# Two-layer diffusion backbone on one core: context halves of the gated tiles and the retention's token tiles moved by 192 bytes, output tiles taken in twos, weight casts tied behind two copies

## The chip, the cores and the metric

The kernel runs on one core of one Trainium2 chip. The metric is the device time of one execution in microseconds (us), as the median of several runs. A core has a matrix engine (TensorE, PE in the profile, with its weight loads listed as PEld), a vector engine (VectorE, DVE), a scalar engine (ScalarE, ACT), a general engine (GpSimd, POOL) and a queue that issues most DMAs (SyncE, SP). Each engine works through its own list of instructions in order and waits at an instruction until the semaphores that it needs have come.

## The reference

Two layers over 512 latent tokens (`x`) and 256 context tokens (`ctx`), width 1024, float32. Layer 0 mixes tokens by windowed attention, layer 1 by bidirectional chunkwise retention with four heads. Each layer ends with the same kind of feed-forward block, of width 2816, that is, 22 feature tiles of 128:

```python
def swiglu(h, w_in, w_out):
    gate, up = jnp.split(h @ w_in, 2, axis=-1)
    return (jax.nn.silu(gate) * up) @ w_out

for i in range(DEPTH):                      # DEPTH = 2
    need_ctx_out = i < DEPTH - 1            # the context leaves the net after layer 0
    h_x, h_c = modulate(rms_norm(x, ...)), modulate(rms_norm(y_ctx, ...))
    out_c, out_x = windowed_gqa_sink(...) if i % 2 == 0 else bidir_retention(...)
    x = x + mx[2] * out_x
    x = x + mx[5] * swiglu(modulate(rms_norm(x, norm2_g[i]), mx[3], mx[4]), ffn_w_in[i], ffn_w_out[i])
    if need_ctx_out:
        y_ctx = y_ctx + mc[2] * out_c
        y_ctx = y_ctx + mc[5] * swiglu(modulate(rms_norm(y_ctx, ...), mc[3], mc[4]), ffn_w_in[i], ffn_w_out[i])
```

So the first feed-forward block works on 512 latent and 256 context tokens, the second one on the 512 latent tokens alone, and the retention's projections work on the latent tokens and read the context's.

## The kernel before

**Products in three.** Every float32 number is held as two parts of a reduced type: a rounded one ("hi", a ScalarE copy that casts) and the rest ("lo", a VectorE subtraction). `split` makes both; `mm3` multiplies them as three matmuls, hi·hi, lo·hi and hi·lo. A weight tile is loaded by SP into a `wraw` buffer and split into `whi` and `wlo` (`next_w`, `w_parts`). Of `wraw` there are two buffers in the pool `rp`; SP's next load into one of them waits until the split of what it held is over.

**Layout.** Each pool of tiles lies at consecutive addresses of a partition, pools on the left and on the right are stacked against each other, and within a pool the tags follow each other in the order of their first use. The sizes are multiples of 256 bytes nearly everywhere. Tiles that start at a multiple of 256 bytes are called on the grid here. `off_grid(pool, cols)` puts a filler of 48 or 16 columns (192 or 64 bytes) into a pool, and so moves the tiles behind it, or on the right side those in front of it, by 192 bytes past the grid; a filler of the other size puts what follows back on it. In the kernel before, the operands of the second feed-forward block (`hx`, `sA`), the token sums of the retention (`sA` in the pool `hS`) and the context's normed tokens (`hc`) stand 192 bytes past the grid; the gated parts of the first feed-forward block (`act`) and the retention's own tokens (`aq` in the pool `hR`: `h_first`, four tiles with the first 256 tokens of the first four feature tiles, and `h_rest`, eight tiles) stand on it.

**First feed-forward block** (lines 879 to 1155, about 380 to 895 us). The 22 feature tiles come in groups of 2, 4, 4, 4, 4 and 4. From the third tile on, `seven` makes gate and up projection with seven quarter products over 384 columns each instead of eight (the 768 tokens are two halves of 384: latent 0 to 383, then latent 384 to 511 with the 256 of the context). `finish_half` multiplies gate and up of one half and splits the product into a part of the tile `act`, which holds hi in columns 0 to 767 and lo in columns 768 to 1535. After the first tile of a group, `output` multiplies the tiles of the group before with `w_out`: for each of the 8 output tiles `d` first the 512 latent columns into a `pj` bank, then the 256 context columns into a `Z` bank, each followed by `gated_add` on VectorE (line 256). One weight tile serves `1024 / (128 * tiles of the group)` output tiles. The last group's output runs all latent tiles first and then all context tiles. Between them `ada_next` hands VectorE one or two sums for the layer-1 modulation, whose weights GpSimd's queue loads.

**Retention** (lines 1159 to 1662). For every head `product_q` streams tokens as the moving operand (256 columns) past weights, and `product_v` streams weights (512 columns) past the tokens as the stationary operand; `quarter_of` says which tiles "11", "12" and "22" (the tokens themselves) and 1 to 4 (the sums) are.

**Second feed-forward block** (lines 1669 to 1785, about 1400 to 1744 us). The same groups, for 512 latent columns. `seven` runs its products in this order: "11" into bank Y, 1 into Z, 2 added to Y, "12" into X, 3 added to Y, 4 added to Z, "22" added to Y. Four ScalarE copies take intermediate states out of the banks: `p1` (line 1720) after "11", `z1` (1722) after 1, `u2` (1724) after 2, `u3` (1729) after 3; product 2 cannot start before `p1` is out of Y. Right after the `p1` copy, `act_parts` splits the gated tile of the seven before. `output` of the group before follows the first `seven` of a group, with four weight tiles for groups of four; the last group's output follows the 22nd tile.

**Order.** The program gives the order in which work is traced; a planner then orders each engine's instructions with estimates of its own for how long each instruction and transfer takes, so a ready instruction may pass one that it thinks is not ready. `after(ins, others)` forbids `ins` to be put ahead of `others` on its engine, and adds no semaphore.

Of the kernel before, what the change touches and what calls it, by code (L numbers as in the profile page):

```python
# [9 lines left out]
F32R = mybir.dt.float32r  # L10
# [4 lines left out]
P = 128  # L15
D = 1024
KT = D // P
SX = 512
SC = 256
# [5 lines left out]
FFN_GROUPS = (2, 4, 4, 4, 4, 4)  # L25
# [24 lines left out]
def dit_kernel(ctx, tc, xT, cT, crow, small, consts, masks, tabs0, tabs1, jtab, adaQ, adaN, adaT, wst, out):  # L50
    nc = tc.nc
# [10 lines left out]
    def T(pool, cols, tag, bufs, dt=F32):  # L62
        return pool.tile([P, cols], dt, tag=tag, bufs=bufs, name=tag)
# [56 lines left out]
    def w_raw(pool=None, bufs=2):  # L120
        raw = T(pool or rp, 1024, "wraw", bufs)
        nc.sync.dma_start(raw, wst[wpos[0]])
        wpos[0] += 1
        return raw

    def w_parts(pool, own=2):

        bufs = own
        if ring:
            pool, bufs = ring[wsel[0] % len(ring)], 2  # L130
        elif wsel[0] % (2 + own) < 2:
            pool, bufs = rp, 2
        wsel[0] += 1
        return T(pool, 1024, "whi", bufs, F32R), T(pool, 1024, "wlo", bufs, F32R)

    def next_w(pool, own=2, raw=None, behind=(), late=()):

        raw = raw or w_raw()
        w = w_parts(pool, own)
        after(split(raw, *w, behind), late)  # L140
        return w
# [21 lines left out]
    def split(t, hi, lo, behind=()):  # L163
        after(nc.scalar.copy(hi, t), behind)  # L164
        return nc.vector.tensor_tensor(lo, t, hi, op=sub)  # L165
# [57 lines left out]
    hpool = [None, None]  # L223
# [4 lines left out]
    def off_grid(pool, cols):  # L228

        nc.gpsimd.memset(T(pool, cols, "off%d" % cols, 1), 0.0)  # L230
# [597 lines left out]
    for g in range(NKV):  # L828
        final = g == NKV - 1
        for i, (s, b) in enumerate((latent + context, latent + context, mixed, late)[g]):  # L830
# [4 lines left out]
            if (g, i) >= SPLIT_AT:  # L835
# [3 lines left out]
                if first:  # L839
                    wo0 = wpos[0]  # L840
                    cres = load_stream(1)
# [5 lines left out]
    xr = load_stream(0)  # L847
# [2 lines left out]
    PLAIN = 2  # L850
    WIDE = SX + SC
    THIRDS = (slice(0, 384), slice(384, WIDE))
    E = ExitStack()
    ep = E.enter_context(tc.tile_pool(name="ep", bufs=1, reuse_waits="tile"))
    wo_p = A.enter_context(tc.tile_pool(name="wo", bufs=1, reuse_waits="tile"))
    wsel[0] = 2
    ada_wo = [(part, d) for part in (3, 4) for d in range(4, KT)]
    for d4 in range(0, KT, 4):
        wpos[0] = wo0 + max(d4, 2)
        w = [next_w(wo_p) if d > 1 else wo_w[d] for d in range(d4, d4 + 4)]  # L860
# [42 lines left out]
    fp = F.enter_context(tc.tile_pool(name="fp", bufs=1, reuse_waits="tile"))  # L903
    quarter = lambda: T(hq, 768, "aq", 20, F32R)
    parts = lambda t: (t[:, 0:384], t[:, 384:768])
    bank = lambda n: T(psF, 512, n, 2)[:, 0:384]
    fp32 = [T(ep, 2 * WIDE, "act", 5) for _ in range(4)]
    tm = [fp32[k % 4][:, k // 4 * WIDE:(k // 4 + 1) * WIDE] for k in range(KT)]
    A = {(k, 0): parts(T(ep, 768, "aq", 8, F32R)) for k in range(KT)}
    A.update({(k, 1): parts(quarter()) for k in range(KT)})  # L910
# [1 line left out]
    def latent_shape():  # L912

        h1 = THIRDS[0]
        for k in range(KT):
# [8 lines left out]
    def context_shape(behind):  # L924
        rms(1, behind=behind)
        for k in range(KT):
            for s, c in ((0, slice(384, SX)), (1, slice(SX, WIDE))):
# [6 lines left out]
                else:  # L934
                    after(ins, [last_shape])
            split(tm[k][:, THIRDS[1]], *A[k, 1])

    park = T(fp, 2048, "crow", 1)

    def token_sums():  # L940

        h1, h2 = THIRDS
        for k in range(4):
# [18 lines left out]
               **{n: (lambda k, n=n: S[n, k]) for n in (1, 2, 3, 4)}}  # L962

    def new_act():
        return T(ep, 2 * WIDE, "act", 5, F32R)

    def finish_half(a, i, t, up):
        nc.vector.tensor_tensor(t, t, up, op=mult)
        c = THIRDS[i]
        return split(t, a[:, c], a[:, c.start + WIDE:c.stop + WIDE])  # L970

    def project_half(w, i, tag):
        o = bank(tag)
# [76 lines left out]
        silu(c21, Y)  # L1050
        return a, finish_half(a, 1, c21, c22)

    streams = ((0, xr, slice(0, SX)), (1, cres, slice(SX, WIDE)))
    ctx_sum = []

    def square_and_stats(s, d, t):
# [18 lines left out]
    def output(acts, final):  # L1075
        gsz = len(acts)
        nd = 1024 // (gsz * P)
        w = []

        def one(s, res, c, d):  # L1080
            while len(w) * nd <= d:
                w.append(spare_w() if final and len(w) == 2 else next_w(fp, 1, raw_turn()))
            wd = w[d // nd]
            o = bank("X" if final else "Z")[:, 0:SC] if s else pj()
            for k in range(gsz):
                c0 = k * nd * P + (d % nd) * P
                mm3(o, (wd[0][:, c0:c0 + P], wd[1][:, c0:c0 + P]),
                    (acts[k][:, c], acts[k][:, c.start + WIDE:c.stop + WIDE]), k == 0, k == gsz - 1)
            ins = gated_add(s, 0, 5, d, o, res)
            if cr and not final and s == 0 and d % 2:  # L1090
                ada_next(ins)
            if final:
                square_and_stats(s, d, res[d])

        if final:
            for st in streams:
                for d in range(KT):
                    one(*st, d)
        else:
            for d in range(KT):  # L1100
                for st in streams:
                    one(*st, d)

    def unit(u):
        w = [T(hq, 768, "aq", 20)[:, 0:512] for _ in range(KT - 4 * (u == 11))]
# [9 lines left out]
    ada_q = [t for i, both in enumerate(ada_both) for t in (both, *ada_one[2 * i:2 * i + 2])]  # L1115
    wsel[0] = 0
    raws = [0]
    cr = None
    last_shape, shape_end = latent_shape()
    first = first_two([next_w(fp, 1), next_w(fp, 1)], [next_w(fp, 1, late=[shape_end]), spare_w([shape_end])])  # L1120
# [4 lines left out]
    f, prev = 0, None  # L1125
    for gsz in FFN_GROUPS:
        acts = []
        for i in range(gsz):
            if f < PLAIN:
                acts.append(first[f])  # L1130
                if f == 1:
                    ends.pop(0)()
            else:
                if f == PLAIN:
                    last_sum()
                a, end = seven()
                acts.append(a)
                if f == PLAIN:
                    ends.pop(0)()
                if f == 4:  # L1140
                    cr = cond_rows(fp)
                if f > 3 and (i or f == 6):
                    ada_next(end)
            if i == 0 and prev is not None:
                output(prev, False)
            f += 1
        prev = acts
# [7 lines left out]
    F.close()  # L1155
    E.close()

# [8 lines left out]
    hS = H.enter_context(tc.tile_pool(name="hS", bufs=1, reuse_waits="tile", side="right"))  # L1166
# [5 lines left out]
    hpool[1] = qp  # L1172
    off_grid(qp, 48)
    h_sum = [(T(hS, 512, "sA", 16, F32R), T(hS, 512, "sA", 16, F32R)) for _ in range(KT)]
    off_grid(hS, 16)
    h_first = [T(hpool[0], 512, "aq", 12, F32R) for _ in range(4)]
    h_rest = [(T(hpool[0], 512, "aq", 12, F32R), T(hpool[0], 512, "aq", 12, F32R)) for _ in range(4)]
    chunk_base = wpos[0]

    def chunk(i, own=False):  # L1180
# [159 lines left out]
    for hd in range(RH):  # L1340
# [24 lines left out]
        Y, X, kc = W4("Y"), W4("X"), W4("X")  # L1365
# [219 lines left out]
        w = []  # L1585
# [82 lines left out]
    fp = F.enter_context(tc.tile_pool(name="fp", bufs=1, reuse_waits="tile"))  # L1668
# [36 lines left out]
    def seven():  # L1705
        g, u = w_raw(fp, 2), w_raw()
        b11 = w_parts(fp, 4)
        b22 = T(hM, 512, "hm", 8, F32R), T(hM, 512, "hm", 8, F32R)
        b14, b32 = w_parts(fp, 4), w_parts(fp, 4)
        split(g, *b11, norm_end)  # L1710
        split(u[:, 512:1024], *b22, norm_end)
        quarter_sums(g, u, first_end[1:2])
        split(u, *b32, first_adds)
        split(g, *b14, first_adds)
        X, Y, Z = (T(psF, 512, n, 2)[:, 0:SC] for n in "XYZ")
        t, up = t_hn(SX), t_sq(SX)
        e1, e2 = T(rp, 512, "res", 12), T(rp, 512, "res", 12)
        p1, z1, u2, u3 = e1[:, HALVES[0]], e1[:, HALVES[1]], e2[:, HALVES[0]], e2[:, HALVES[1]]
        product(Y, operand_a("11"), b11, 0, True)
        act_parts([nc.scalar.copy(p1, Y)])  # L1720
        product(Z, operand_a(1), b14, 0, True)
        nc.scalar.copy(z1, Z)
        product(Y, operand_a(2), b32, 512, False)
        nc.scalar.copy(u2, Y)
        product(X, operand_a("12"), b11, 512, True)
        nc.vector.tensor_tensor(t[:, HALVES[0]], p1, X, op=add)
        silu(t[:, HALVES[0]], t[:, HALVES[0]])
        product(Y, operand_a(3), b32, 0, False)
        nc.scalar.copy(u3, Y)
        product(Z, operand_a(4), b22, 0, False)  # L1730
        nc.vector.tensor_tensor(up[:, HALVES[0]], u2, Z, op=add)
        product(Y, operand_a("22"), b14, 512, False)
        nc.vector.tensor_tensor(up[:, HALVES[1]], u3, z1, op=add)
        silu(t[:, HALVES[1]], Y)
        nc.vector.tensor_tensor(t, t, up, op=mult)
        act = new_act()
        pending.append((t, *act))
        return act

    pending = []  # L1740

    def act_parts(behind=()):
        while pending:
# [2 lines left out]
    def output(acts, final):  # L1746
        gsz = len(acts)
        nd = 1024 // (gsz * P)
        w = []
        for d in range(KT):  # L1750
            while len(w) * nd <= d:
                w.append(next_w(fp, 4))
            wd = w[d // nd]
            o = pj()
            for k in range(gsz):
                c0 = k * nd * P + (d % nd) * P
                mm3(o, (wd[0][:, c0:c0 + P], wd[1][:, c0:c0 + P]), acts[k], k == 0, k == gsz - 1)
            ins = gated_add(0, 1, 5, d, o, xr)
            if len(first_adds) < 2:
                first_adds.append(ins)  # L1760
                after(first_mult[2], [ins])
            if final:
                nc.sync.dma_start(out[:, d, :], xr[d])
# [3 lines left out]
    for gsz in FFN_GROUPS:  # L1767
        acts = []
        for i in range(gsz):
            if f < 2:  # L1770
                acts.append(first[f])
            elif f == 2:
                w = [next_w(fp, behind=norm_end) for _ in range(2)]
# [155 lines left out]
```

## Time and profile before

| what | us |
|---|---|
| three runs | 1748.04 median, 1747.25 to 1749.0 |
| the profiled execution: its own time | 1746.27 |
| span of the profiled execution | 1744.5 |
| TensorE busy in the span | 1706.8 (98%) |
| VectorE busy | 1351.3 (77%) |
| ScalarE busy | 847.1 (49%) |

The granted TensorE clock is 0.999 of full speed. The profile's first part gives busy times by engine, its fourth the chain of work that ended last, its fifth groups of equal instructions. A row of groups reads: line, engine, operation, tile written and tiles read, shape, count, then busy time and mean duration of one in ns, then the idle time of the engine just before them and what ended it. A row of the timeline reads: start, duration, engine, line, operation, tiles, shape, count, and in brackets idle time before it with what ended it. A matmul's duration includes some 165 ns in which the next one already runs, so its rate is read from start to start.

### The profile page before, as it was taken

To read this page: it belongs to the slowest core of one execution; us is meant where nothing else is said; L and a number is where in the kernel's file an instruction comes from. 1 tells how busy PE (TensorE), PEld (TensorE's weight loads), DVE (VectorE), ACT (ScalarE), POOL (GpSimd) and SP (SyncE) were. 2 spreads that over 40 slices of the span, in tenths; PEclk is the share of its full clock that TensorE was granted. 3 is DMA by queue.
4 is the path that set the end of the run, shared out by engine and by line. 5 is a ranking of instruction groups with operands and counts; after the bars stand their busy time and mean duration, and the time that the engine had idled before them with its cause. 6 is when DMAs were issued, how large, how long until landed. Compare 5 with 4: busy or idle time off the path is not lost.

```text
span 1744.5 us, 27601 instructions
## 1 busy us (share of the span) xinstructions
PE 1706.8 (98%) x10876; PEld 1516.0 (87%) x10876; DVE 1351.3 (77%) x2368; ACT 847.1 (49%) x1492; POOL 132.2 (8%) x272
## 2 busy tenths in 40 slices
PE   7999999999999999999999999999999999999998
PEld 5777877899999999999988788898898899989987
DVE  6687778788778788787889858858768798877774
ACT  5476667455433334342556534525525565445442
POOL 0034435000000000000000000000000000000000
PEclk9999999999999999999999999999999999999999
DMA  9501012534243434343433524524423224233322
GB/s 350 233 13 38 13 43 68 198 120 142 71 147 121 158 109 145 122 151 103 154 102 87 181 76 132 166 82 125 160 86 114 80 79 133 80 113 106 106 76 85
DMA packets 59603, 203.54 MB, mean 117 GB/s; under 512 B 6609, under 2 KB 6993, under 8 KB 59217
## 3 DMA queue, kind: packets, MB, share of 16 engines
q1 hardware_dynamic: 51984, 175.03, 30.2%
q0 software_dynamic: 7200, 26.22, 4.9%
q8 instruction: 85, 1.39, 0.3%
q10 hardware_dynamic: 288, 0.52, 0.1%
q14 instruction: 46, 0.37, 0.1%
HBM read 199.65 MB, written 2.10 MB: 116 GB/s over the span
## 4 chain that ended last, share of the span: by engine, by line
PE 70%; DVE 14%; DMA 7%; ACT 4%; issue 3%; POOL 1%; SPq 0%; ACTq 0%; DVEq 0%; POOLq 0%
PE Y L886 13%; PE pj L147 6%; PE pj L148 6%; PE pj L149 6%; PE Z L886 6%; DMA wraw<-in_wst_dram 4%; PE Z L1270 4%; PE X L886 3%; DVE wlo L165 3%; PE pT L726 2%; PE pO L740 2%; PE S L703 2%; ACT whi L164 1%; PE X L1259 1%; PE Y L1259 1%
## 5 line engine op out<-in xcount | busy, mean ns | idle before, releaser
L164 ACT CAST whi<-wraw 128x1024 fp32r<-128x1024 f32 x258 | 270.2, 1051 | 373.1 <-PE Z L149 86.9
L165 DVE TENSOR_TENSOR wlo<-wraw,whi 128x1024 fp32r<-128x1024 f32 x258 | 315.3, 1225 | 61.7 <-ACT whi L164 59.1
L886 PE MATMUL Y<-aq,whi 128*128 128x384 f32 x640 | 173.7, 335 | 0.3 <-ACT hn L1035 0.3
L256 DVE SCALAR_TENSOR_TENSOR res<-pj,mod,res 128x512 f32<-128x512 f32 (+1 forms) x112 | 81.6, 730 | 64.9 <-PE pj L149 64.4
L886 PEld LDWEIGHTS Y<-aq,whi 128*128 128x128 f32 x640 | 116.7, 188 | 1.6 <-ACT hn L1035 1.4
L273 DVE CUSTOM_DVE_ANT_0 y<-adaw,crow,small_sb 128x1024 bf16<-128x1024 f32 x64 | 82.0, 1281 | 38.6 <-DMA adaw<-in_adaT_dram 38.3
L886 PE MATMUL Y<-aq,wlo 128*128 128x384 f32 x320 | 107.0, 334 | 0.0
L101 ACT ACTIVATE pr<-pr,stat,qs 128x513 f32<-128x513 f32 (+2 forms) x96 | 74.4, 777 | 22.8 <-DVE stat L710 22.2
L1270 PE MATMUL Z<-whi,sA 128*128 128x512 f32 x256 | 81.6, 393 | 1.6 <-ACT gate L1456 1.6
L717 POOL TENSOR_SCALAR pr<-pr,stat 128x512 f32<-128x512 f32 (+2 forms) x96 | 71.2, 755 | 78.7 <-DVE stat L714 54.0
L147 PE MATMUL pj<-ax,whi 128*128 128x512 f32 x176 | 68.7, 391 | 0.9 <-DVE res L256 0.9
L149 PE MATMUL pj<-ax,whi 128*128 128x512 f32 x176 | 68.7, 390 | 0.0
L148 PE MATMUL pj<-ax,wlo 128*128 128x512 f32 x176 | 68.6, 390 | 0.0
L147 PE MATMUL pj<-act,whi 128*128 128x512 f32 x168 | 66.0, 393 | 0.0
L148 PE MATMUL pj<-act,wlo 128*128 128x512 f32 x168 | 65.9, 392 | 0.0
L149 PE MATMUL pj<-act,whi 128*128 128x512 f32 x168 | 65.5, 390 | 0.0
L270 POOL DMA_DIRECT2D adaw<-in_adaT_dram x48 | 25.6, 533 | 514.6 <-DVE mod L273 413.1
L886 PE MATMUL Y<-sA,whi 128*128 128x256 f32 x304 | 59.1, 280 | 4.8 <-ACT res L1720 4.1
L726 PE MATMUL pT<-const_sb,pr 128*128 128x128 f32 x352 | 57.0, 283 | 6.9 <-POOL pr L717 4.6
L886 PEld LDWEIGHTS Y<-aq,wlo 128*128 128x128 f32 x320 | 60.1, 188 | 0.0
L726 PEld LDWEIGHTS pT<-const_sb,pr 128*128 128x128 f32 x352 | 38.5, 140 | 24.2 <-POOL pr L717 13.6
L1270 PEld LDWEIGHTS Z<-whi,sA 128*128 128x128 f32 x256 | 48.0, 188 | 13.2 <-ACT gate L1456 2.8
(576 smaller groups left out, 5141.8 us busy)
## 6 DMA issues: line engine op xcount, KB each, us to landing
wraw<-in_wst_dram SPq DMA_DIRECT2D x224, 512.0 KB, 3.7
adaw<-in_adaT_dram POOLq DMA_DIRECT2D x48, 512.0 KB, 3.8
wx<-in_wst_dram SPq DMA_DIRECT2D x30, 512.0 KB, 4.3
adan<-in_adaQ_dram SPq DMA_DIRECT2D x16, 512.0 KB, 7.8
adan<-in_adaN_dram SPq DMA_DIRECT2D x12, 512.0 KB, 7.6
adaw<-in_adaT_dram SPq DMA_DIRECT2D x8, 512.0 KB, 3.8
res<-in_xT_dram SPq DMA_DIRECT2D x14, 256.0 KB, 3.1
aq<-in_adaN_dram SPq DMA_DIRECT2D x12, 256.0 KB, 5.8
```

The costliest lines, as they stand in the source:

```text
L101: ins = nc.scalar.activation(*args, **kw)
L147: nc.tensor.matmul(o, whi, xhi, start=first, stop=False)
L148: nc.tensor.matmul(o, wlo, xhi, start=False, stop=False)
L149: return nc.tensor.matmul(o, whi, xlo, start=False, stop=last)
L164: after(nc.scalar.copy(hi, t), behind)
L165: return nc.vector.tensor_tensor(lo, t, hi, op=sub)
L256: return nc.vector.scalar_tensor_tensor(res[d], o, mods[l, s][:, part, d:d + 1], res[d], mult, add)
L273: res.append(nc.vector.tensor_tensor_reduce(junk, w, cr[:, s * 1024:(s + 1) * 1024], 1.0, sm_t[:, C_ADAB + l * 48 + j:C_ADAB + l * 48 + j ...
L717: nc.gpsimd.tensor_scalar(pt[:, :n], pt[:, :n], st[:, 6 + e:7 + e], 1.0, op0=mult, op1=mult)
L726: nc.tensor.transpose(tp[:, a * P:(a + 1) * P], self.pr[(0, 2, 1, 3)[a]][:, ki * P:(ki + 1) * P], ident)
L886: nc.tensor.matmul(o, p, r, start=first and k + i == 0, stop=k == 3 and i == 2, skip_group_check=not first)
L1270: ins = nc.tensor.matmul(os[t], p, r, start=first and k + i == 0, stop=k == 3 and i == 2, skip_group_check=by_k or not first)
```

## The change

Four edits:

1. The tile `act` of the first feed-forward block grows from 1536 to 1600 columns. The latent tokens' hi and lo parts lie in columns 0 to 511 and 512 to 1023; the context's hi and lo parts follow at column 1024 in the first tile of a group, and 48 columns (192 bytes) further in the others. `finish_half` of the second half therefore makes two splits, of 128 and of 256 columns, where it made one of 384.
2. `output` of that block, except for the last group, takes the output tiles in twos: the latent parts of two tiles, then the context parts of the same two.
3. In the retention's pool `hR` the 64-byte filler that stood in the pool `hS` now stands behind eleven `aq` tiles: all of `h_rest` and the last three tiles of `h_first` get 192 bytes past the grid, `h_first[0]` gets a tag of its own and stays on it, and the tiles of `hS` stay where they were.
4. In the second feed-forward block, `output` may put the cast of its first weight tile only behind the `z1` copy and that of the second one only behind the `u2` copy of the seven traced before it.

```diff
+    ACT = 1600
...
-    fp32 = [T(ep, 2 * WIDE, "act", 5) for _ in range(4)]
+    fp32 = [T(ep, ACT, "act", 5) for _ in range(4)]
...
     def new_act():
-        return T(ep, 2 * WIDE, "act", 5, F32R)
+        a = T(ep, ACT, "act", 5, F32R)
+        c0 = 2 * SX + 48 * (made[0] > 0)
+        made[0] = (made[0] + 1) % made[1]
+        return (a[:, 0:SX], a[:, SX:2 * SX]), (a[:, c0:c0 + SC], a[:, c0 + SC:c0 + 2 * SC])
+
+    made = [0, 0]
 
     def finish_half(a, i, t, up):
         nc.vector.tensor_tensor(t, t, up, op=mult)
-        c = THIRDS[i]
-        return split(t, a[:, c], a[:, c.start + WIDE:c.stop + WIDE])
+        if i == 0:
+            return split(t, *(p[:, 0:384] for p in a[0]))
+        split(t[:, 0:P], *(p[:, 384:SX] for p in a[0]))
+        return split(t[:, P:384], *a[1])
...
-                mm3(o, (wd[0][:, c0:c0 + P], wd[1][:, c0:c0 + P]),
-                    (acts[k][:, c], acts[k][:, c.start + WIDE:c.stop + WIDE]), k == 0, k == gsz - 1)
+                mm3(o, (wd[0][:, c0:c0 + P], wd[1][:, c0:c0 + P]),
+                    acts[k][s], k == 0, k == gsz - 1)
...
-            for d in range(KT):
+            for d0 in range(0, KT, 2):
                 for st in streams:
-                    one(*st, d)
+                    for d in (d0, d0 + 1):
+                        one(*st, d)
...
+    made[:] = 0, FFN_GROUPS[0]
...
     for gsz in FFN_GROUPS:
         acts = []
+        made[:] = 0, gsz
...
-    off_grid(hS, 16)
-    h_first = [T(hpool[0], 512, "aq", 12, F32R) for _ in range(4)]
-    h_rest = [(T(hpool[0], 512, "aq", 12, F32R), T(hpool[0], 512, "aq", 12, F32R)) for _ in range(4)]
+    h_rest = [(T(hpool[0], 512, "aq", 11, F32R), T(hpool[0], 512, "aq", 11, F32R)) for _ in range(4)]
+    h_first = [T(hpool[0], 512, "aq", 11, F32R) for _ in range(3)]
+    off_grid(hpool[0], 16)
+    h_first.insert(0, T(hpool[0], 512, "aq0", 1, F32R))
...
-        nc.scalar.copy(z1, Z)
+        copies[:] = [nc.scalar.copy(z1, Z)]
...
-        nc.scalar.copy(u2, Y)
+        copies.append(nc.scalar.copy(u2, Y))
...
-    pending = []
+    pending, copies = [], []
...
-                w.append(next_w(fp, 4))
+                w.append(next_w(fp, 4, behind=copies[len(w):len(w) + 1]))
```

More of the change, by code (lines that the diff above doesn't have):

```diff
@@ L1051, in seven @@
         return a, finish_half(a, 1, c21, c22)
-    streams = ((0, xr, slice(0, SX)), (1, cres, slice(SX, WIDE)))
+    streams = ((0, xr), (1, cres))
     ctx_sum = []
@@ L1078, in output, with one @@
         w = []
-        def one(s, res, c, d):
+        def one(s, res, d):
             while len(w) * nd <= d:
```

## The prediction

> **What bounds the kernel now.** I read the page's first part, then the busy time of a long stretch, then TensorE's waits.
>
> ```profile
> PE 1706.8 (98%) x10876; PEld 1516.0 (87%) x10876; DVE 1351.3 (77%) x2368; ACT 847.1 (49%) x1492; POOL 132.2 (8%) x272
> ```
> ```profile
> 440.00:860.00 420.00, 419.68 (x2411) 401.60 (x2409) 330.58 (x499) 159.23 (x247) 25.08 (x49) 1.00 0.41 129
> ```
>
> The stretch's columns are its bounds and length, then busy time of PE, PEld, DVE, ACT, POOL, clock, DMA. Most of the first feed-forward block (420 us shown) leaves TensorE 0.3 us idle: there only the rate of the matmuls can be bettered, and VectorE has 420 - 330.58 = 89 us to spare. TensorE's waits in the second block (1440 to 1744 us; total, times, longest), and below them those of the first block in that stretch:
>
> ```profile
> PE Y L886 <- ACT res L1720: 4.1, 5, 1.1
> PE Y L886 <- ACT res L1724: 0.7, 1, 0.7
> ```
> ```profile
> PE Y L886 <- ACT hn L1035: 0.3, 2, 0.2
> ```
>
> So nearly all that the second block's products wait for is one copy, `p1` (line 1720), five times. The timeline of the second of these places, with the load that it turns on, and then TensorE's wait at the last one:
>
> ```profile
> 1531.53 0.33 SPq L122 DMA_DIRECT2D wraw<-in_wst_dram  x1
> ```
> ```profile
> 1534.45 0.28 PE L886 MATMUL Z<-sA,whi 128*128 128x256 f32 x1
> ...
> 1535.68 1.04 ACT L164 CAST whi<-wraw 128x1024 fp32r<-128x1024 f32 x1 [1.08 <-DMA wraw<-in_wst_dram]
> 1535.70 0.28 PE L886 MATMUL Z<-sA,whi 128*128 128x256 f32 x1
> 1536.63 0.36 ACT L1720 COPY res<-Y 128x256 f32<-128x256 f32 x1
> 1536.75 1.22 DVE L165 TENSOR_TENSOR wlo<-wraw,whi 128x1024 fp32r<-128x1024 f32 x1 [0.90 <-ACT whi L164]
> ...
> 1537.05 0.38 PE L886 MATMUL Y<-sA,whi 128*128 128x256 f32 x1 [1.07 <-ACT res L1720]
> ...
> 1537.27 0.28 PE L886 MATMUL Y<-sA,wlo 128*128 128x256 f32 x1
> ```
> ```profile
> 1544.67 0.39 PE L147 MATMUL pj<-ax,whi 128*128 128x512 f32 x1
> ...
> 1546.71 0.39 PE L147 MATMUL pj<-ax,whi 128*128 128x512 f32 x1
> ```
> ```profile
> 1711.01 0.38 PE L886 MATMUL Y<-sA,whi 128*128 128x256 f32 x1 [0.35 <-ACT res L1720]
> ```
>
> This is the first seven of a group. Product "11" has left Y when Z's first matmul has started (1534.45, plus its tail), so `p1` could run at 1534.6. But ScalarE, which works in order, stands before the cast of the output's third weight tile, whose load was issued at 1531.53 and lands 4.15 us later. The copy comes 2.0 us late; the product between covers part; TensorE pauses from 1535.70 to 1537.05, 1.35 us where 0.12 is usual. The matmul at 1544.67 is the output's fourth, so the output began at 1544.0; nine more take it to 1546.71, 0.227 us each.
>
> **Part 1, tied casts.** Removed: the five waits. 4.1 us idle, plus the tail of about 0.165 us that each row still counts as busy, is 4.9 us; the matmul after a pause takes 0.22 us to the next (1537.05 to 1537.27) instead of 0.11, five times 0.1. Together 5.4 us. How it goes: the first cast now waits for `z1`. The third weight's load needs the first weight's buffer, so the third cast cannot stand before `p1` any more, whatever the planner thinks of transfers. With `p1` at 1534.6 and products of 12 x 0.113 = 1.36 us, `z1` ends about 1536.4, first cast 1537.3, `u2` 1537.8, second cast 1538.8, subtraction of the first (1.22) 1538.6. What is queued behind: the third load goes out at 1538.6 instead of 1531.53, lands at 1542.7 by today's 4.15, is split by 1545.1. The seven ends 1.3 us earlier than 1544.0, at 1542.7; the output wants its first weight then (4 us to spare) and its third after four tiles of 12 x 0.227 us, at 1553.6 (8 us). SP's next load into that buffer, the second half of the next seven's weights, waits for the same subtraction: it moves from 1538.0 (1536.75 + 1.22) to 1545.1, lands at 1549.3, and needs its splits and sums: casts of 0.6 and 1.04, subtractions of 0.7 and 1.22, four half-width sums of 0.7 (the half widths by the rows of part 3), with five gated additions between,
>
> ```profile
> L256 DVE SCALAR_TENSOR_TENSOR res<-pj,mod,res 128x512 f32<-128x512 f32 (+1 forms) x112 | 81.6, 730 | 64.9 <-PE pj L149 64.4
> ```
>
> some 10 us, so ready about 1559.4. The output's eight tiles last until 1564.5: 5 us to spare, and if that cover were gone the next seven would start later by as much. The fifth place is the last tile, before the closing output: its pause is 0.5 us (0.35 and the tail), and there the late weights' subtraction (1.22) may stand before that of the last gated tile, which TensorE wants at once. I take that place at nothing (between +0.6 gained and 1.2 lost): the part gives **4.8 us** (3.6 to 5.4).
>
> **Part 2, 192 bytes.** Groups by form, from the whole run:
>
> ```profile
> L1270 PE MATMUL Z<-wlo,sA 128*128 128x512 f32 x128 | 50.6, 395 | 0.0
> ...
> L1270 PE MATMUL Z<-whi,aq 128*128 128x512 f32 x128 | 41.7, 393 | 0.0
> ...
> L149 PE MATMUL Z<-act,whi 128*128 128x256 f32 x144 | 40.7, 283 | 0.0
> ...
> L886 PE MATMUL Z<-sA,hm 128*128 128x256 f32 x228 | 29.1, 277 | 0.0
> ...
> L1259 PE MATMUL Y<-aq,whi 128*128 128x256 f32 x128 | 24.2, 282 | 0.0
> ```
>
> At 256 columns those that stream tiles on the grid (`act`, `aq`) take 282 to 283 ns, those past it (`sA`) 277, with weights on the grid in both: 6 ns. The starts say the same, and show something more:
>
> ```profile
> 606.08 0.28 PE L147 MATMUL Z<-act,whi 128*128 128x256 f32 x1
> ...
> 607.51 0.40 PE L147 MATMUL pj<-act,whi 128*128 128x512 f32 x1
> 607.75 0.40 PE L148 MATMUL pj<-act,wlo 128*128 128x512 f32 x1
> ...
> 610.26 0.28 PE L147 MATMUL Z<-act,whi 128*128 128x256 f32 x1
> ```
> ```profile
> 1705.04 1.52 PE L886 MATMUL Z<-sA,hm 128*128 128x256 f32 x12
> 1706.40 0.28 PE L886 MATMUL Y<-hx,whi 128*128 128x256 f32 x1
> ```
>
> Twelve on the grid: 1.43 us (119 ns each). Twelve past it: 1.36 us (113 ns). And the twelve 512-column matmuls after a context tile on the grid take 2.75 us where 12 x 0.227 = 2.72: each return to the latent tokens costs about 0.03 us.
>
> First block: a context tile of a group of four keeps three matmuls on the grid and moves nine: 9 x 5.7 = 0.05 us; output tiles in twos halve the returns, 0.013 us a tile. Four outputs of 8 tiles: 32 x 0.063 = 2.0. The group of two: 8 x (3 x 5.7 ns + 0.013) = 0.25. The closing output: 8 x 0.05 = 0.4. Together **2.65 us**; should the returns vanish and the three go fast too, 3.6; with a rate in between, 1.3.
>
> Retention: of 288 `product_q` matmuls over the tokens 264 move (`h_first[0]` serves 6 a head): 264 x 6 = 1.6 us. Against it, the same tiles are the stationary operand of 288 `product_v` matmuls, and there the row past the grid (`sA`, 395) is dearer than the one on it (`aq`, 393): 264 x 2 = 0.5 lost. Net **1.1** (0 to 1.6).
>
> The Trainium skill speaks against this part: SBUF — State Buffer, "Who interferes with whom", gives TensorE two independent read ports, one for the moving operand and one for weights, and says that PE and ACT "never wait on anyone". By that, where a tile starts would change nothing, and the sum would be the casts' alone. The trace does not agree: 119 against 113 ns at the same shape, with nothing waited for.
>
> **Part 3, what is added.** Each of 22 gated tiles gets one more cast and one more subtraction:
>
> ```profile
> L164 ACT CAST act<-hn 128x384 fp32r<-128x384 f32 x19 | 9.8, 515 | 11.4 <-DVE hn L968 11.0
> ```
> ```profile
> L165 DVE TENSOR_TENSOR act<-sq,act 128x384 fp32r<-128x384 f32 x19 | 10.5, 553 | 0.0
> ```
>
> From 1024 columns (1.04 and 1.22 us, rows above) to 384 a cast loses 0.53 us and a subtraction 0.67, so what does not hang on the width is 0.20 and 0.15 us: 22 times that is 4.4 us of ScalarE and 3.3 of VectorE, under the 89 us that VectorE idles beside matmuls. I cost it at nothing; uncovered at every tile it would be up to 7.7 us, and -0.2 is possible at the closing output, which now gets its last latent part from a 128-column split. Twos leave the banks' turnover as it is: between two uses of a `pj` bank lie one latent and two context tiles in either order, of a `Z` bank two latent and one. SP's loads and GpSimd's queue keep their order in this block, and the moved filler is the same GpSimd instruction in another pool. `act` grows by 1,280 bytes for five buffers, on the grid, so what follows moves by whole steps.
>
> **Sum.** 4.8 + 2.65 + 1.1 = 8.55 us. The profiled execution took 1746.27 (span 1744.5 and 1.8 around it), 1.8 under the median of 1748.04; to 1737.7 on its scale, **1739.5** on the median's.
>
> **Rivals.** All start from 1739.5.
> (a) The 192 bytes do nothing, as by the rule above: 3.75 less, 1743.2. Only an unseen cause of the 6 ns speaks for it.
> (b) The tie moves the pause: the first cast (1.05) now stands before `u2` and holds product 3 instead. For it: the copies are 1.4 us apart. Against: product "12" runs between and gives 1.36 us. 4.8 less, 1744.3, on the border of what counts as faster.
> (c) The planner, with new pieces in every tile of the first block, orders casts before the copies of line 1035. Today this happens twice for 0.3 us idle; with tail and restart some 0.43 us each, in 20 sevens 8.6 us: 1748.1, no change.
> (d) Slower: the third cast, now late, is put before `u3` (line 1729). Its load lands at 1542.7, so `u3` would end at 1544.1, while product "22" (the seven's last 1.36) wants it at 1541.3: a pause of 2.8 us plus 0.1, in five places 14.5: 1754.0. It decides if the planner believes a load of this kind lands before product 3 ends (two products earlier, 1540.0), 1.4 us after its issue; today it believed less than 3.1 us (1531.53 to 1534.6), the truth being 4.15.
>
> **How the numbers follow.** My forecast 0.66, (a) 0.06, (b) 0.08, (c) 0.08, (d) 0.12. 0.2% is 3.5 us, about what a measurement of this kernel can tell from no change: under 1744.5 faster, over 1751.5 slower. Faster: 0.66 + 0.06 + half of (b) = 0.76; same 0.12; slower 0.12. The forecast's own range is 1737.4 (all parts at their best, 10.6) to 1743.1 (4.9, all at their worst); runs spread by 1 us, and the other waits above (0.7, 0.3) may go: low end 1735.5. The high end, 1747.0, takes in (a) and (b) and leaves (c) and (d), 0.20, out.
>
> **What would show it.** The wait for line 1720 gone or under 0.5 us, and no new one for 1722 to 1729; `Z<-act` rows near 278 and `Y<-aq` rows near 277 ns, `Z<-whi,aq` up by 2; the first block still without idle time. Wrong: waits for VectorE's `wlo` at the outputs of the second block, a growing wait for line 1035, or rows at 283.

## The result and the profile after

| | us |
|---|---|
| before | 1748.04 median of 15 runs (1746.36 to 1750.13) |
| changed | 1744.19 median of 15 runs (1741.41 to 1746.21) |
| ratio | 0.9979, 95% interval 0.9972 to 0.9986 |

The change is faster by 0.21%, 3.85 us by the medians (2.4 to 4.9 by the interval), where 8.55 us were forecast. Of the changed kernel, the page's busy times and the long stretch of the first feed-forward block:

```profile
PE 1707.1 (98%) x10876; PEld 1513.4 (87%) x10876; DVE 1354.3 (78%) x2390; ACT 849.9 (49%) x1514; POOL 131.1 (8%) x272
```
```profile
440.00:860.00 420.00, 419.77 (x2419) 401.72 (x2418) 335.25 (x521) 161.80 (x268) 25.02 (x49) 1.00 0.43 130
```

The stretch is as full as before (0.23 us idle), and VectorE has 335 us in it instead of 331: the added pieces. TensorE's waits from 1440 us on (total, times, longest):

```profile
PE pj L147 <- DVE res L256: 2.7, 6, 0.5
PE pj L147 <- ACT ax L164: 0.9, 1, 0.9
PE Y L887 <- ACT res L1736: 0.4, 1, 0.4
```

The five waits for `p1` (now line 1732) are gone, all 4.1 us of them. In their place stand six waits at a place where there was none: at the output tiles, for the gated addition of line 256. What the 192 bytes did, in the groups by form:

```profile
L1282 PE MATMUL Z<-whi,aq 128*128 128x512 f32 x128 | 41.8, 394 | 0.0
...
L147 PE MATMUL Z<-act,whi 128*128 128x256 f32 x144 | 40.2, 279 | 0.0
L148 PE MATMUL Z<-act,wlo 128*128 128x256 f32 x144 | 40.0, 278 | 0.0
...
L1271 PE MATMUL Y<-aq,whi 128*128 128x256 f32 x128 | 23.4, 278 | 0.0
```

The rows that stream the moved tiles, 281 to 283 ns before, are at 278 to 279, near the 277 to 278 of the forecast; the row that holds moved tiles as weights (`Z<-whi,aq`) rose from 393 to 394, where 395 was forecast.

Tails (the end of a matmul that still counts as busy while TensorE already waits) and restarts (the longer interval of the first matmul behind a pause) hide in such rows, so I also worked out from every trace how TensorE's time splits. From each matmul's start to the next one's start is its interval; when it is over 0.08 us longer than is usual for its width (0.227 us at 512 columns, 0.114 at 256), what exceeds the usual is a pause; the rest is rate. "First block" runs from about 414 to 881 us of the kernel before, "retention" from 896 to 1396, "second block" from 1432 to 1740, each between the same two matmuls in all kernels. Sums in us; rows with a count are means over the traces of the kernels that share the edit:

| | first block: rate + pauses | retention: rate + pauses | second block |
|---|---|---|---|
| before | 465.30 + 1.40 | 488.71 + 10.68 | 308.58 |
| changed | 462.80 + 1.69 | 487.65 + 12.50 | 308.02 |
| before and the kernels below without any of the edits to that part | 465.26 + 1.22 (6) | 488.72 + 11.32 (9) | 309.00 (7) |
| changed and the kernels below with all of them | 462.82 + 1.64 (4) | 487.85 + 12.54 (5) | 308.30 (2, both ties) |

So by the means the first block gave 2.0 us (rate -2.44, pauses +0.42), the retention nothing (-0.87 and +1.22), the second block 0.7. Traces that are alike in a part lie up to 0.6 us from their mean in the first block, up to 0.9 in the retention and up to 1.6 in the second block (308.3 to 310.6 without ties), and up to 2 us in the part before 410 us, which the change does not touch. The first block's gain stands clear of that; the 0.7 of the second block can't be told from nothing.

How the gain of the missing `p1` waits is lost again is seen at the second block's second output. Of the changed kernel, ScalarE and then VectorE and TensorE there, and last VectorE at the same output of the kernel before:

```profile
1533.21 0.37 ACT L1732 COPY res<-Y 128x256 f32<-128x256 f32 x1 [0.99 <-PE Y L887]
1533.48 0.62 ACT L164 CAST ax<-hn 128x512 fp32r<-128x512 f32 x1
1534.57 0.37 ACT L1734 COPY res<-Z 128x256 f32<-128x256 f32 x1 [0.47 <-PE Z L887]
1534.84 1.05 ACT L164 CAST whi<-wraw 128x1024 fp32r<-128x1024 f32 x1
1535.93 0.38 ACT L1736 COPY res<-Y 128x256 f32<-128x256 f32 x1
1536.20 1.05 ACT L164 CAST whi<-wraw 128x1024 fp32r<-128x1024 f32 x1
...
1543.31 1.05 ACT L164 CAST whi<-wraw 128x1024 fp32r<-128x1024 f32 x1 [1.23 <-DMA wraw<-in_wst_dram]
```
```profile
1551.83 0.68 DVE L896 TENSOR_TENSOR wraw<-wraw 128x512 f32<-128x512 f32 x1
1552.45 2.41 DVE L165 TENSOR_TENSOR wlo<-wraw,whi 128x1024 fp32r<-128x1024 f32 x2
1554.77 0.75 DVE L256 SCALAR_TENSOR_TENSOR res<-pj,mod,res 128x512 f32<-128x512 f32 x1
```
```profile
1552.83 0.40 PE L147 MATMUL pj<-ax,whi 128*128 128x512 f32 x1
...
1554.67 0.39 PE L149 MATMUL pj<-ax,whi 128*128 128x512 f32 x1
1555.57 0.50 PE L147 MATMUL pj<-ax,whi 128*128 128x512 f32 x1 [0.51 <-DVE res L256]
```
```profile
1550.60 2.36 DVE L165 TENSOR_TENSOR wlo<-wraw,whi 128x1024 fp32r<-128x1024 f32 x2 [0.22 <-ACT whi L164]
1552.88 0.74 DVE L256 SCALAR_TENSOR_TENSOR res<-pj,mod,res 128x512 f32<-128x512 f32 x1
1555.07 0.75 DVE L256 SCALAR_TENSOR_TENSOR res<-pj,mod,res 128x512 f32<-128x512 f32 x1 [1.44 <-PE pj L149]
```

The first two casts stand behind `z1` and `u2` as tied, and `p1` runs as soon as TensorE lets it. But the output's fourth weight is split from 1543.31 on, inside the output (which begins at 1541.17), and so is all that follows it in the `wraw` buffers. The output's fourth tile is complete when the fifth begins (1552.83, plus the tail of its last matmul); its gated addition, which frees the bank that the sixth tile needs (there are two `pj` banks), starts only at 1554.77, behind two subtractions (2.41 us together) of the next `seven`'s weights. TensorE starts the sixth tile at 1555.57, 0.90 us after the last start, where 0.23 is usual. In the kernel before, the two subtractions run one tile earlier (from 1550.60), and VectorE is idle for 1.44 us before the fourth addition (1555.07): there it waits for TensorE.

### The profile page after: what moved, and what is told of

Same layout as the page of the kernel before. It is cut to its first block, busy times and chain, and to the rows that moved or that the text cites. A ratio compares the mean times of both kernels' runs of the same rounds, so it can differ in the third digit from the quotient of the medians.

```text
span 1742.2 us, 27645 instructions
## 1 busy us (share of the span) xinstructions
PE 1707.1 (98%) x10876; PEld 1513.4 (87%) x10876; DVE 1354.3 (78%) x2390; ACT 849.9 (49%) x1514; POOL 131.1 (8%) x272
## 4 chain that ended last, share of the span: by engine, by line
PE 65%; DVE 16%; DMA 9%; ACT 4%; issue 3%; POOL 1%; SPq 0%; ACTq 0%; DVEq 0%; POOLq 0%
PE Y L887 13%; PE Z L887 6%; DMA wraw<-in_wst_dram 6%; PE pj L147 5%; PE pj L148 5%; PE pj L149 5%; DVE wlo L165 4%; PE Z L1282 4%; PE X L887 3%; PE pT L726 2%; PE S L703 2%; PE pO L740 2%; PE X L1271 1%; PE Y L1271 1%; DMA adan<-in_adaQ_dram 1%
```

## The experiments

Ratios are to the kernel before, measured on the same chip beside each, with 95% intervals. Theory A: the ties cost what they gain because they bunch VectorE's work in the output.

**Both ties alone.** Edit 4 on the kernel before.

```diff
-                w.append(next_w(fp, 4))
+                w.append(next_w(fp, 4, behind=copies[len(w):len(w) + 1]))
```

> The kernel before with the ties of edit 4 alone. Theory A (late loads bunch VectorE's work): the ties take the five waits for p1 away (5.4 us with tails and restarts), but they hold back the loads of the third and fourth output weights, VectorE then splits these and the next seven's weights in one stretch inside the output, and the gated addition that frees a pj bank stands behind two subtractions; 4 to 5 us come back. So 0.3 to 1.0 us less than before (about 1747.4), with waits of TensorE for line 256 of about 3.4 us in 6 or 7 places. Rival B (the waits for line 256 come from the moved tiles, not from the ties): 4 to 5.5 us less, about 1743.2, and no waits for line 256 beyond the one of the kernel before (0.9).

Measured: 0.9988 (0.9980 to 0.9997). The waits from 1440 us on:

```profile
PE pj L147 <- DVE res L256: 3.0, 7, 0.6
PE Y L886 <- ACT res L1724: 0.7, 1, 0.7
PE pj L147 <- ACT ax L164: 0.5, 1, 0.5
```

The waits for line 256 come with the ties alone, so B falls. The second block took 308.58 us in this trace, as in that of the kernel before. The timed gain, 0.5 to 3.5 us, is somewhat more than A's 0.3 to 1.0 but below B's 4.

**All but the ties.** Edits 1 to 3.

```diff
-                w.append(next_w(fp, 4, behind=copies[len(w):len(w) + 1]))
+                w.append(next_w(fp, 4))
```

> The changed kernel without the ties of edit 4: the 192 bytes and the twos remain. Theory A: what is left is the rate in the first block (2.2 us in the trace of the changed kernel) and in the retention (0.9 by the rates, less what weights come late by chance): 2 to 3.2 us less than before, about 1745.4; five waits for p1 as before, no wait for line 256 beyond 0.9. Rival B: waits for line 256 stay and the kernel is 1 us or more slower than before.

Measured: 0.9983 (0.9974 to 0.9991), 3.0 us. The waits for `p1` are back:

```profile
PE Y L887 <- ACT res L1732: 5.3, 5, 1.5
```

They stand in five places as before, and from 1440 us on TensorE does not wait for line 256. Most of what the change brought stays without the ties.

**Another tie: the third cast behind `p1`.** What held `p1` up was the cast of the output's third weight alone. Here only that cast is tied, and the first two stay early.

```diff
-        act_parts([nc.scalar.copy(p1, Y)])
+        copies[:] = [nc.scalar.copy(p1, Y)]
+        act_parts(copies)
...
-                w.append(next_w(fp, 4))
+                w.append(next_w(fp, 4, behind=copies if len(w) == 2 else ()))
```

> The kernel before with another tie: only the cast of an output's third weight is put behind the p1 copy, the first two casts stay as early as they are, so no load comes later. Theory A: the cast waits for its load anyway, so VectorE's work stays spread; the five waits for p1 go and no new ones come: 4.5 to 5.4 us less than before, about 1743.1. Rival C (VectorE has no room in that stretch, so any pause that is taken away comes back at the gated additions): less than 1.5 us gained, and new waits for line 256.

Measured: 0.9966 (0.9952 to 0.9979), 5.9 us by the ratio; the second block took 304.77 us, 4.2 under the mean without a tie. The waits from 1440 us on:

```profile
PE Y L886 <- ACT res L1720: 1.2, 3, 0.5
PE Y L886 <- ACT res L1725: 0.4, 1, 0.4
PE Y L886 <- ACT res L1730: 0.2, 1, 0.2
```

C falls: VectorE has room when its work stays spread, and the pause does not come back at line 256. But three waits for `p1`, which A did not expect, are new. They are one `seven` later, where TensorE, now early, meets a cast that waits for its load (at 1567.78 the cast into `hm`, which holds the weights of product 4; `p1` runs at 1568.30).

**That tie in the changed kernel**, in place of its own two: the same lines.

> The changed kernel with this tie (third cast behind the p1 copy) in place of its own two. Theory A: the gains add up, 7 to 8.6 us less than before, about 1740.3, that is some 4 us less than the changed kernel. Rival C: no more than 1 us less than the changed kernel (1744.2).

Measured: 0.9961 (0.9948 to 0.9973), 6.8 us; second block 305.72, first block 462.87 + 1.88. A's lower end is just missed, C's 1 us is exceeded. The two gains add up in part, within what these intervals can tell.

**The first tie alone.**

```diff
-                w.append(next_w(fp, 4))
+                w.append(next_w(fp, 4, behind=copies[:1] if not w else ()))
```

> The kernel before with half of edit 4: only the output's first weight cast is put behind the z1 copy. Theory A (what harms is that the third weight's load, which needs the first weight's buffer, goes out some 6 us later): the second block is as with both ties, within 1 us of the kernel before there, no wait for p1 and about 3.4 us of waits for line 256. Rival D (both loads have to come late for VectorE to be crowded): the waits for line 256 fall under 2 us and the second block gets 2 us or more shorter than with both ties.

Measured: 0.9991 (0.9982 to 1.0000); second block 306.36, 2.2 us less than in the trace with both ties.

```profile
PE pj L147 <- DVE res L256: 1.4, 4, 0.5
PE Y L886 <- ACT res L1724: 0.8, 1, 0.8
PE pj L147 <- ACT ax L164: 0.3, 1, 0.3
```

By this trace about half of the harm, within D's numbers and not A's: each tie brings its share. The times can't show it (1.6 us less than before with one tie, 2.1 with both, each give or take 1.5). VectorE's order in the output is the same as with both; the pause before the sixth tile is 0.43 to 0.47 us in three of four places where both ties have 0.7.

**The ties, with the gated addition put first.** No work is taken away; only two subtractions may not pass the fourth tile's addition.

```diff
-        split(u, *b32, first_adds)
-        split(g, *b14, first_adds)
+        after(split(u, *b32, first_adds), hold)
+        after(split(g, *b14, first_adds), hold)
...
             ins = gated_add(0, 1, 5, d, o, xr)
+            if d == 3:
+                hold[:] = [ins]
```

> The kernel before with edit 4, and the two subtractions of the next seven's late weights (b32, b14) may stand only behind the gated addition of the output's fourth tile. No work is removed. Theory A1 (the pause is one of order: the planner put two subtractions of 1.23 us ahead of an addition that frees a bank): the four pauses of about 0.7 us before the sixth tile go, with their restarts some 3 us: second block 2.5 to 3.2 us shorter than with the ties alone, about 1744. Rival C (VectorE has no room there): the pauses only move, to the seventh and eighth tile or to the next seven's weights; less than 1 us gained.

Measured: 0.9974 (0.9963 to 0.9985), 4.5 us; second block 303.97, 4.6 us less than with the ties alone. VectorE at the second output, and the waits from 1440 us on:

```profile
1553.60 0.68 DVE L895 TENSOR_TENSOR wraw<-wraw 128x512 f32<-128x512 f32 x1
1554.27 0.75 DVE L256 SCALAR_TENSOR_TENSOR res<-pj,mod,res 128x512 f32<-128x512 f32 x1
1554.94 2.35 DVE L165 TENSOR_TENSOR wlo<-wraw,whi 128x1024 fp32r<-128x1024 f32 x2
```
```profile
PE pj L147 <- DVE res L256: 0.7, 2, 0.5
PE pj L147 <- ACT ax L164: 0.6, 1, 0.6
```

The addition now stands ahead of the two subtractions, the pauses before the sixth tile are gone in all four places, and nothing took their place. So it was the order on VectorE and not its load: with the same work and the same late loads, the second block is 5.0 us under the mean without ties. That the planner chose the order because it reckoned the late loads' subtractions to be ready by then is likely, but not shown. By the traces more came back than A1's 3.2 us (the wait for line 1724, 0.7, went too); by the times it is 2.4 us more than the ties alone gave.

**A version faster than both the kernel before and the changed one.** The changed kernel with the third cast behind `p1` instead of its ties, and each cast into `hm` behind the `p1` of the third `seven` before it.

```diff
-        split(u[:, 512:1024], *b22, norm_end)
+        split(u[:, 512:1024], *b22, [*norm_end, *p1s[-3:-2]])
...
         act_parts(copies)
+        p1s.append(copies[0])
```

> The changed kernel with the third cast behind p1 in place of its two ties, and in addition the hm cast of each seven put behind the p1 copy of the third seven before it: in the trace with the third cast tied, this cast, which waits for its load, holds up p1 of the second seven of a group in three places (0.5 us each, 0.7 with tail and restart). If that is the whole reason, the three go: 2 us less than with the third cast tied alone, about 1741.5, and 6 to 8 us less than before. If TensorE is then only early for something else, less than 0.7 us and a wait of another name.

Measured: 1740.16 us median against 1748.38, ratio 0.9953 (0.9940 to 0.9966), 8.2 us; second block 303.14, 2.6 less than with the third cast's tie in the changed kernel.

```profile
PE Y L887 <- ACT res L1743: 0.6, 1, 0.6
PE Y L887 <- ACT res L1738: 0.6, 1, 0.6
```

No wait for `p1` is left; two single waits for `u3` and `u2` are, 1.2 us together. The interval lies below that of the changed kernel (0.9972 to 0.9986); from the third cast's tie alone (0.9948 to 0.9973) the times can't tell it.

**Edit 1 alone:** the 192 bytes, output tiles in ones (the diff of edit 1 above, without edit 2).

> The kernel before with edit 1 alone: the context parts of three of four gated tiles 192 bytes past the grid, one more cast and subtraction a tile, output tiles in ones. If the moving operand's address sets the rate (256 columns: 114 against 120 ns), the first block's products outside pauses fall by 9 x 5.7 ns in 32 tiles and less in the others, 2.2 us by the prediction's working; pauses there stay as they are. If the twos made the gain, less than 0.7 us.

Measured: 0.9994 (0.9985 to 1.0003). The rate is 463.24 us, 2.06 less, so the address makes the gain; but pauses took 2.71 instead of 1.40, and only 0.75 is left in the block. The largest share is waits for the copies of line 1035 of the kernel before (here line 1043), 1.0 us idle where it was 0.3; the prediction's rival (c) named them, if for the change as a whole and in 20 places. In the stretch from 440 to 880 us:

```profile
PE Y L887 <- ACT hn L1043: 1.0, 2, 0.8
```

**The twos alone** (edit 2).

> The kernel before with edit 2 alone: output tiles of the first block in twos. It halves the returns from 256 to 512 columns, 16 of the 32 in the groups of four and 4 in the group of two, 0.027 us each: the products outside pauses fall by 0.5 us, from 465.3 to 464.8, with no new pause. If the return costs nothing by itself, no change.

Measured: 0.9992 (0.9983 to 1.0001); rate 464.92, 0.38 less than before (expected 0.5), pauses 1.03. With edit 1 the twos bring the rate to 462.80 and the pauses back to 1.2 to 1.9 in four traces. Why they shorten the pauses I did not test.

**The added pieces alone:** two splits instead of one, all on the grid.

```diff
-        c0 = 2 * SX + 48 * (made[0] > 0)
+        c0 = 2 * SX + 0 * (made[0] > 0)
```

> The kernel before with the form of edit 1 but without its 192 bytes: every tile's context parts stay on the grid, the second half of a tile is split in two as in the change, output tiles in ones. It costs only what is added. If the added casts and subtractions are hidden, the first block's products outside pauses take 465.3 us as before (address theory: with the 192 bytes 463.2) and its pauses stay at 0.8 to 1.4. If the pauses of the kernel with edit 1 alone (2.7) come from the added pieces, they are 2 us or more here too.

Measured: 1.0011 (1.0002 to 1.0020), slower by 0.3 to 3.5 us; rate 465.16, pauses 1.96, 0.7 more than the mean without it and just under the 2 us that would have put the pauses of edit 1 on the pieces. Most of the 7.7 us of added work is hidden, not all, and the 192 bytes, not the split, make the rate. The execution traced was the shortest of ten, so it may show too few pauses.

**All context tiles past the grid**, the first of a group too.

```diff
-        c0 = 2 * SX + 48 * (made[0] > 0)
+        c0 = 2 * SX + 48
```

> The kernel before with edit 1, but the context parts of all tiles, the first of a group too, 192 bytes past the grid; output tiles in ones. By the prediction's rate the three matmuls more per context tile give 3 x 5.7 ns x 40 = 0.7 us more than edit 1 alone (products outside pauses 462.5 against 463.2), and up to 1.8 us more if the return to 512 columns is then free as well (461.4). Rival F (a change from 512 columns on the grid to 256 past it costs something of its own, which the first tile on the grid avoids): 463.2 or more.

Measured: 0.9999 (0.9990 to 1.0008); rate 463.52, pauses 3.36. The rate is within F's bound: three more matmuls past the grid gained nothing against edit 1 alone (463.24). All twelve now run at one middle speed, shown in the last section; a row of this kernel:

```profile
L147 PE MATMUL Z<-act,whi 128*128 128x256 f32 x144 | 40.5, 281 | 0.0
```

**Retention alone** (edit 3).

> The kernel before with edit 3 alone (eleven token tiles of the retention 192 bytes past the grid). The prediction's step: 1.1 us less. Rival E (the retention's pace is set where TensorE waits for a weight's split, so matmuls that run faster only wait longer): the products outside pauses take 1.0 us less, as in the four traces with this edit (487.65 to 488.24 against 488.71 to 488.91), and the pauses take 0.7 to 1.2 us more (11.0 to 12.0 became 11.6 to 13.1), so the time is that of before within 0.5 us, 0.03%.

Measured: 0.9996 (0.9987 to 1.0005); rate 487.77, 0.94 less than before, pauses 13.32, 2.6 more (2.0 over the mean without). Its waits from 895 to 1395 us, and those of the kernel before:

```profile
PE Z L1271 <- DVE wlo L165: 0.8, 2, 0.4
...
PE Y L1260 <- DVE wlo L165: 0.7, 1, 0.7
```
```profile
PE Y L1259 <- DVE wlo L165: 0.5, 1, 0.5
...
PE Z L1270 <- DVE wlo L165: 0.4, 1, 0.4
```

E holds by the traces; the times alone can't decide, as their interval (2.3 us less to 0.9 more) has room for the forecast's 1.1 as well. Over the five traces with the edit and the nine without, five places where TensorE waits for a weight's split took the time back: pauses there went from 0.71 us to 0.92, 0.00 to 0.09, 0.43 to 0.74, 0.06 to 0.22 and 0.26 to 0.56, together 1.07 of the 1.22 us by which the pauses grew. VectorE's and ScalarE's order in those places did not change: products that run faster reach the same weights earlier and wait for them.

## Why the prediction was wrong

**Part 1, tied casts (forecast 4.8, measured 0.7 in the traces).** The wait was priced about rightly: with the same two ties and the addition put first the second block fell by 5.0 us, and with the third cast's own tie by 3.3 and 4.2, in spite of three new waits. What failed is the step "What is queued behind". It followed the late loads to the next `seven` and found "5 us to spare", and that held: from 1440 us on TensorE waits for no weight. But it counted the "five gated additions between" only as time that VectorE needs, not as work that TensorE waits for two tiles later. So the cover was looked for at the end of the output, when TensorE was already held up at the sixth tile, by the fourth tile's addition. The load did come as late as the prediction let it (issued at 1537.18, 4.0 us behind the start of `p1`, where the kernel before issued it 5.1 us ahead of it), and the prediction named waits at the outputs as a sign, but for `wlo`, not for line 256. None of the rivals was this one: (b) and (d) looked for the new pause at the copies, where nothing new appeared (the 0.4 us at `u2` were 0.7 before). That the time, 1744.19, came out next to (b)'s 1744.3 is chance as to the place: (b) has the right kind, a tie that moves the pause, on the wrong engine.

The last tile, taken "at nothing (between +0.6 gained and 1.2 lost)", was a small loss: its `p1` pause of 0.6 went, and the pause at the closing output, 0.28 with restart before, became 1.15.

**Part 2, 192 bytes and twos (forecast 2.65 and 1.1).** By rate 2.44 (within the 1.3 to 3.6 given) and 0.87: the mechanism held and rival (a) fell. The Trainium skill's SBUF — State Buffer, "Who interferes with whom", gives the moving operand and the weights read ports of their own; what the prediction read from it, that an address would change nothing, the traces again do not bear out (119 to 120 ns on the grid, 113 to 114 past it behind others). The pauses took 0.42 us of the first block's gain back. In the retention both halves of the rate came out as worked out: matmuls that stream the moved tiles took 1.54 us less (1.6 forecast), those that hold them as weights 0.55 more (0.5 forecast), and other rows moved by 0.1. The retention's 1.1 failed all the same, because the rate was counted as time, although the kernel before showed waits for weights in that very stretch, and a wait with a fixed end swallows what is gained ahead of it. There the term should have been near 0.

The upper end of part 2, "should the returns vanish and the three go fast too, 3.6", was not to be had by moving the three as well: with all twelve past the grid the returns do vanish (15 ns a tile gained), but the three stay as they were (353 ns together against 352) and the other nine get slower, by some 20 ns.

**Part 3, what is added.** Costed at nothing; by the trace of the pieces alone some 0.7 us, by its times 0.3 to 3.5.

**The sum.** 0.7 + 2.0 - 0.35 = 2.4 us by the traces, the low end of the 2.4 to 4.9 by the times. The range (1735.5 to 1747.0) holds 1744.19 only because its high end was drawn to take in (a) and (b); the forecast's own range ended at 1743.1. "Faster" was right, but 3.85 us came of 8.55, and 4.1 of the 6.2 us that the traces miss lie in part 1, 1.45 in the retention, 0.6 in the first block.

## What to carry to other kernels

Before a cast is held back, ask which buffer its subtraction frees, which load starts then, and where the load's own work lands on the next engine's list; above all, whether something that frees a bank stands behind it. To take one late instruction out of the way of a copy, tie that instruction, not the two before it; if they are tied, put the additions that free a bank first. A faster rate counts only as far as the next wait whose end does not depend on it: in the first block, with hardly a wait, it was worth 2.0 of 2.4 us, in the retention nothing.

## What the runs showed of the hardware

How fast a 256-column matmul with its moving tile past the grid runs depends, in these traces, on what ran before it. Median intervals in the first block, with the weights on the grid in all of them, from start to start:

| context tile | first three matmuls | fourth to sixth | the other six | first six at 512 columns after it |
|---|---|---|---|---|
| all on the grid (before) | 114, 119, 120 ns | 120, 120, 120 | 120 | 233, 236, 228, 233, 231, 226 |
| three on, nine past it (edit 1 alone) | 113, 119, 120 | 121, 122, 116 | 113 to 114 | 232, 233, 231, 227, 227, 227 |
| all past it | 118, 118, 118 | 118, 117, 118 | 117 to 118 | 227 each |

Behind three matmuls on the grid the others reach 113 ns; straight after 512-column ones the same tiles stay at 118 for all twelve, and then the return to 512 columns costs nothing.

The second block of the kernel before shows the same two paces. Not all of `hx` stands past the grid there: its first tile, `hx0`, lies on the other side of the filler, on the grid. Where a `seven` starts with it behind an output (1504.44), the intervals are 113, 119, 120, 121, 122, 116 and then 113 to 114. Where later tiles of `hx` follow 512-column matmuls directly (1442.79), the next 41 intervals are 117 to 119 ns, until one of 120 and one of 161; some matmuls later they are 113 to 114. Behind a longer pause either follows: 113 to 114 behind one of 0.86 us (1458.21), 117 to 119 behind one of 0.77 (1475.46). The free return does not carry over: behind the latter, the first intervals at 512 columns (from 1482.63) are 233, 234, 236, 224, 230 and 236 ns. What in the chip keeps this state from one matmul to the next the runs don't show.
